# The second block of a two-block layer rebuilt: state rows exchanged by TensorE, queries and keys with features on partitions, attention output normed with tokens on partitions

## The chip, the cores and the metric

The kernel runs on one core of a Trainium2 chip. A core has TensorE (PE), VectorE (DVE), ScalarE (ACT), GpSimd (POOL) and SyncE (SP), which only issues transfers here. The metric is the device time of one launch in microseconds; the median of the runs counts. The profile is of one execution.

## The reference, cut to what matters

Two transformer blocks run on 512 tokens of width 1024 in fp32. The first is a hybrid of four token mixers with a gated FFN. The second, on which the change works, is this, with a modulated norm before each half:

```python
h = _rms(x, norm1_w) * (1 + sc1) + sh1
u, q, k, v = jnp.split(h @ w_in, [512, 1024, 1152], axis=-1)
y_ssm = _s5(u, ...)            # 32 groups of 16 channels, 64 complex states
q = _rms(q.reshape(b, s, 8, 64), q_norm_w)      # per head
k = _rms(k.reshape(b, s, 2, 64), k_norm_w)
y_attn = _swa_sink(q, k, v, rel_bias, sinks)    # window 128, blocks of 128 queries
mixed = jnp.concatenate([_rms(y_ssm, out_norm_ssm), _rms(y_attn, out_norm_attn)], axis=-1)
x = x + g1 * (mixed @ w_out)
h2 = _rms(x, norm2_w) * (1 + sc2) + sh2
x = x + g2 * _conv_ffn(h2, w_up, conv_w, conv_b, w_down)

# _s5: s[t] = a * s[t-1] + B u[t] (complex), y = Re(C s) + D * u
z = jax.nn.gelu(y)
return z * jax.nn.sigmoid(z @ w_glu + b_glu)

# _swa_sink, per head and query block of 128 over 256 keys
m = max(max(logits), sink); p = exp(logits - m)
out = (p / (sum(p) + exp(sink - m))) @ v
```

## The kernel before

A matrix product in fp32 accuracy is three passes of TensorE: each operand is split into a high and a low part (whi, wlo for weights, the two halves of an hl tile for activations), and hi·hi, lo·hi, hi·lo are added in PSUM. `proj_f` (L447) gives 128 output features on partitions by 512 tokens (24 matmuls of 512 columns for a width of 1024), `proj_t` (L476) gives tokens on partitions.

In time the program is: block 1 with its FFN until about 735 us; the middle of block 2 from there to about 940 us; the last FFN to the end. While the first FFN runs, "fillers" (L1227) compute tables for the state-space part (S5) and the modulation vectors.

The middle consists of steps, each a Python function that issues work for all engines. On TensorE the steps run in the order of the string ORDER, under `manual_schedule` (L1648). On the other engines the scheduler places the instructions. The steps, with the letters of ORDER before the change:

- U (`u_last`): the last projection of u. u goes to DRAM (d_u) and comes back as `ua`, 16 loads on POOL's queue, with channels of a group and 8 tokens on partitions.
- a, b, c, d (`s5_a` to `s5_d`), for each quarter q of the 32 groups: `a` multiplies ua by the table et (8 matmuls); `b` rotates the states (VectorE with real and imaginary halves crossed, `crossed`, POOL for one product) and scans them along the chunks of 8 tokens; `c` rotates back; `d` multiplies ua by tt and the states by gt (16 matmuls), sends the result through DRAM (d_z) to bring channels on partitions (yt), and adds D·u.
- e (`s5_e`): gelu and the split for the GLU. g (`glu`): w_glu, sigmoid as tanh, product, sum of squares. R (`norm_s`): the norm's scale.
- kp, qp: keys, values and queries with tokens on partitions; the head norms on VectorE (`head_norm`, L513 to L530, tile tokn); kt, qt: transposes to k2T, q2T.
- s, t, v (`swa_s`, `swa_t`, `swa_v`): for each of 8 pairs of a key head and a query block: scores, bias and row minimum on VectorE (L1577), exponentials on ScalarE (L1584), division on VectorE (L1587), transposes of the probabilities, and the product with v, with output features on partitions. Squares are summed into tot_a.
- p (`ssm_out`): the S5 half of the out-projection plus x, which is loaded again from d_x. A (`norm_a`): the attention norm's scale r_a. Then the attention half (`product`, finished by `w_out2`: scale by r_a on VectorE L1658, add L1659) leads over to the last FFN.

PSUM: three banks "acc", two "sc", two "tr", one "pv" (tile po). The constants NW2, NTAB are numbers of SBUF buffers; EN is a string that says for each copy or square whether ScalarE (a) or VectorE (v) does it.

Of the kernel before, what the change touches and what calls it, by code (L numbers as in the profile page):

```python
# [17 lines left out]
P = 128  # L18
# [23 lines left out]
HP = ""  # L42
EG = 0
EN = "avaaavaaaaaaaaaaaaavvvvvvvavavvaaaavaaaaaaaaaaaavaavvvvavvvvaaaavvvvaavvvaaaaavavaaavaavvavvvvvvvvvvavvaavvvvvavvaaavaaaavaaavvaaaaaaavvvvvvvaaaaaaaaavvvavvaavaaaav"
EN_AT = {'k1': (0, 4), 'v1': (4, 4), 'q1': (8, 12), 'h1': (20, 8), 'w1': (28, 8), 's1': (36, 8), 'o1': (44, 16), 't1': (60, 46), 'u2': (106, 4), 'z2': (110, 4), 'y2': (114, 4), 'k2': (118, 2), 'v2': (120, 2), 'q2': (122, 4), 'h2': (126, 12), 's2': (138, 12), 't2': (150, 14)}
ORDER = "U kp0 kp1 a0 a1 kt0 b0 qp0 c0 a2 b1 qp1 kt1 b2 c1 d0 a3 c2 qt0 qt1 b3 c3 d1 s0 qp2 s1 s2 t0 d2 t1 d3 e0 s3 e1 qt2 t2 s4 qp3 v0 t3 s5 v1 g0 qt3 g1 g2 t4 g3 s6 v2 v3 s7 t5 R p0 p1 v4 p2 t6 v5 p3 p4 v6 t7 p5 v7 p6 p7 A"
# [6 lines left out]
NW2 = 19  # L53
START = {0: lambda wc, wk: (wc[0].load(), wk[0].load())}
KSQ = 4
ZC = "bc"
# [8 lines left out]
def _rng(*r):  # L65
# [59 lines left out]
def pvec(i):  # L125
# [17 lines left out]
    o["ssm_d"] = _fv(z(i["ssm_d_2"])[0])  # L143
# [42 lines left out]
BLOCK1 = ("dist", "nlm", "distc", "rsum", "bd")  # L186
# [14 lines left out]
def arrays_of(i):  # L201
# [9 lines left out]
    for n in ("k", "v"):  # L211
# [9 lines left out]
        [np.concatenate(q) for q in ((br, bi), (bi, br), (cr, ci), (ci, cr))], axis=1))  # L221
    rb = g("rel_bias_2")
# [8 lines left out]
def build(tc, I, out, PV, PVN, CS, CSN, CS1, CSN1):  # L231
# [815 lines left out]
    d_g = [dpool.tile([P, 1152], F32, name=f"d_g{q}") for q in range(4)]  # L1047
# [24 lines left out]
    def s5_tables():  # L1072
# [72 lines left out]
        for n in range(8):  # L1145
            cmul(ro_r[:, n + 1], ro_i[:, n + 1], ro_r[:, n], ro_i[:, n], ro_r[:, n], ro_i[:, n], [P, 32], V)
# [231 lines left out]
    def tab(nm):  # L1378
        return bp.tile([P, 1024], F32, tag="tab", bufs=6, name=nm)
# [365 lines left out]
```

## Time and profile before

| | us |
|---|---|
| median of three runs | 1325.03 |
| lowest and highest | 1323.76, 1325.33 |
| the profiled execution | 1322.91 |
| its span on the core | 1321.2 |
| TensorE busy | 1242.7 (94% of the span) |
| VectorE busy | 840.3 (64%) |
| ScalarE busy | 551.5 (42%) |

The profiled execution is 2.1 us below the median. Its trace gives each instruction with its engine, source line, tile names, shapes and the idle time before it, with what ended that idle time. fp32 matmuls (those that aren't in three passes) count as two instructions each. A start-to-start distance says what an instruction costs in a row of its like; its own duration is longer, since matmuls overlap.

### The profile page before, as it was taken

The numbers are of one execution on the slowest core, as the hardware profiler recorded it, in microseconds if no ns is written. First come the engines' busy times: TensorE is split into PE (matmuls) and PEld (weight loads), VectorE is DVE, ScalarE is ACT, GpSimd is POOL, SyncE is SP. The second block draws the span as 40 slices with busy tenths as digits, with TensorE's granted clock in tenths as the row PEclk, the third lists the DMA queues.
The fourth block names the chain that finished last, engine by engine and source line by source line (L and its number), as shares of the span: only waits on it lengthen the run. The fifth ranks groups of instructions, "written<-read, shape, count | busy, mean of one in ns | idle before, by whom it ended". The sixth has DMA issues, their size and how long they took to land.

```text
span 1321.2 us, 17322 instructions
## 1 busy us (share of the span) xinstructions
PE 1242.7 (94%) x6269; PEld 999.7 (76%) x6269; DVE 840.3 (64%) x1615; ACT 551.5 (42%) x916; POOL 322.5 (24%) x403
## 2 busy tenths in 40 slices
PE   7999999999989879999999997889889999999998
PEld 6888765667867657778888986758868788888887
DVE  7668768777988878745445768775736353434362
ACT  5334466445223112322233442775655544444430
POOL 3000004012327439092511133014121212121200
PEclk8999999999999889999999987889989999999999
DMA  6431111126567676643434775277397979595921
GB/s 214 138 126 49 50 32 49 50 78 198 156 211 243 197 238 197 192 156 109 139 109 157 273 187 156 80 162 145 67 185 139 219 155 188 127 190 124 192 85 64
DMA packets 210869, 192.44 MB, mean 146 GB/s; under 512 B 13024, under 2 KB 173680, under 8 KB 210784
## 3 DMA queue, kind: packets, MB, share of 16 engines
q1 hardware_dynamic: 154240, 146.43, 36.5%
q0 software_dynamic: 51456, 40.61, 19.3%
q10 hardware_dynamic: 5088, 4.29, 1.0%
q8 instruction: 50, 0.82, 0.3%
q14 instruction: 35, 0.29, 0.1%
HBM read 177.70 MB, written 15.43 MB: 146 GB/s over the span
## 4 chain that ended last, share of the span: by engine, by line
PE 53%; DVE 12%; DMA 11%; issue 4%; ACT 2%; POOL 1%; ACTq 0%; DVEq 0%; POOLq 0%
PE acc L259 33%; PE sc L259 10%; PE tr L259 9%; DMA wm<-in_wmod_dram 7%; DVE wm L1065 3%; DVE wlo L371 2%; DMA wlo<-in_w_dram 1%; PE po L259 1%; DMA raw<-in_w_dram 1%; DVE hd L498 1%; DMA ua<-d_u 1%; PE tr L1595 1%; DVE z L1457 1%; DVE z L1446 1%; DVE z L1445 0%
## 5 line engine op out<-in xcount | busy, mean ns | idle before, releaser
L259 PE MATMUL acc<-hl,whi 128*128 128x512 f32 (+1 forms) x1624 | 487.1, 383 | 18.5 <-ACT whi L365 7.2
L259 PEld LDWEIGHTS acc<-hl,whi 128*128 128x128 f32 x1624 | 296.7, 190 | 87.6 <-issue 18.1
L365 ACT ACTIVATE whi<-raw 128x1024 fp32r<-128x1024 f32 (+1 forms) x187 | 193.9, 1039 | 365.8 <-PE acc L259 192.8
L259 PE MATMUL acc<-hl,wlo 128*128 128x512 f32 (+1 forms) x812 | 309.7, 382 | 1.7 <-DMA wlo<-in_w_dram 1.6
L371 DVE TENSOR_TENSOR wlo<-raw,whi 128x1024 fp32r<-128x1024 f32 (+1 forms) x133 | 177.7, 1338 | 61.2 <-ACT whi L365 58.4
L259 PEld LDWEIGHTS acc<-hl,wlo 128*128 128x128 f32 x812 | 153.9, 190 | 33.9 <-issue 4.4
L259 PE MATMUL acc<-hd,whi 128*128 128x512 f32 (+1 forms) x472 | 148.5, 398 | 17.2 <-DVE x L1327 11.0
L369 POOL DMA_DIRECT2D wlo<-in_w_dram x54 | 72.0, 1334 | 320.6 <-ACT wlo L368 216.7
L259 PEld LDWEIGHTS acc<-hd,whi 128*128 128x128 f32 x472 | 89.1, 194 | 40.7 <-DVE x L1327 9.2
L259 PE MATMUL acc<-whi,hl 128*128 128x256 f32 (+1 forms) x544 | 109.0, 291 | 1.9 <-ACT tok L246 1.6
L1065 DVE CUSTOM_DVE_ANT_0 wm<-wm,cb 128x512 f32<-128x512 f32 x96 | 81.1, 864 | 32.5 <-DMA wm<-in_wmod_dram 31.1
L259 PEld LDWEIGHTS acc<-whi,hl 128*128 128x128 f32 x544 | 89.2, 195 | 6.8 <-ACT tok L246 3.0
L259 PE MATMUL acc<-hd,wlo 128*128 128x512 f32 (+1 forms) x236 | 93.5, 396 | 0.0
L259 PE MATMUL acc<-wlo,hl 128*128 128x256 f32 (+1 forms) x272 | 78.9, 290 | 0.5 <-DVE wlo L371 0.5
L259 PE MATMUL tr<-hl,whi 128*128 128x512 f32 (+1 forms) x240 | 74.6, 394 | 0.0
L259 PE MATMUL sc<-hl,whi 128*128 128x512 f32 x208 | 64.9, 393 | 0.0
L368 ACT ACTIVATE wlo<-raw 128x1024 fp32r<-128x1024 f32 x54 | 56.5, 1046 | 3.9 <-PE acc L259 2.0
L259 PEld LDWEIGHTS acc<-wlo,hl 128*128 128x128 f32 x272 | 53.0, 195 | 2.6 <-DVE wlo L371 1.0
L918 POOL TENSOR_SCALAR_AFFINE_SELECT keep<-keep 128x128 f32<-128x128 f32 x16 | 9.3, 594 | 185.1 <-ACT keep L912 184.3
L259 PEld LDWEIGHTS acc<-hd,wlo 128*128 128x128 f32 x236 | 45.8, 194 | 9.9
L259 PEld LDWEIGHTS tr<-hl,whi 128*128 128x128 f32 x240 | 45.7, 193 | 10.1
L259 PE MATMUL tr<-hl,wlo 128*128 128x512 f32 (+1 forms) x120 | 47.5, 396 | 6.1 <-DMA wlo<-in_w_dram 6.1
(423 smaller groups left out, 1957.6 us busy)
## 6 DMA issues: line engine op xcount, KB each, us to landing
raw<-in_w_dram SPq DMA_DIRECT2D x177, 512.0 KB, 4.3
wlo<-in_w_dram POOLq DMA_DIRECT2D x54, 512.0 KB, 7.8
wm<-in_wmod_dram SPq DMA_DIRECT2D x96, 256.0 KB, 4.0
xk<-in_xT_dram SPq DMA_DIRECT2D x16, 256.0 KB, 4.7
d_g<-s5g POOLq DMA_DIRECT2D x4, 576.0 KB, 4.3
gt<-d_g SPq DMA_DIRECT2D x4, 576.0 KB, 5.7
w1c<-in_w1k_dram SPq DMA_DIRECT2D x8, 256.0 KB, 5.3
w1c<-in_w1v_dram SPq DMA_DIRECT2D x8, 256.0 KB, 6.6
```

Of the source, the lines that this page charges most:

```text
L259: nc.tensor.matmul(o, lhsT=l, rhs=r, start=start, stop=stop, **k)
L365: act(hi[:, :m], raw[:, :m], AF.Copy)
L368: act(lo[:, :m], raw[:, :m], AF.Copy, scale=-1.0)
L369: nc.gpsimd.dma_start(v(lo), self.src[:, k0:k1, c0:c1], accum_op=ALU.add)
L371: V.tensor_tensor(lo[:, :m], raw[:, :m], hi.bitcast(F32)[:, :m], op=ALU.subtract)
L498: V.tensor_tensor(dst[:, 1], src, dst.bitcast(F32)[:, 0], op=ALU.subtract)
L918: G.affine_select(g[:, d], g[:, d], fill=1.0, **past)
L1065: V.tensor_tensor_reduce(wm, wm, cb[:, n * 512:(n + 1) * 512], 1.0, 0.0, ALU.mult, ALU.add, mh[:, n, j:j + 1])
L1446: V.scalar_tensor_tensor(dst[im], src[re], -sign, t[re], op0=ALU.mult, op1=ALU.mult)
L1457: V.tensor_tensor_scan(z2[:, c], mag8[:, q * 8 + g:q * 8 + g + 1].to_broadcast([P, 64]), z[:, c], 0.0, ALU.mult, ALU.add)
L1595: nc.tensor.transpose(tp[:, m * P:(m + 1) * P], probs[n][:, hh, (j - j0) * P:(j - j0 + 1) * P], ident)
```

## The change

S5: `a` now makes, beside the states, the same states with real and imaginary halves exchanged, by two matmuls of half height per group. VectorE multiplies both from PSUM by cos and sin, adds, scans, and multiplies by cos and sin again; the return crossing is left out, and `d` instead takes a second product, with a table gs that is gt with its halves exchanged (24 matmuls in place of 16). D·u is put into the table tt by 32 small matmuls in the first FFN's fillers. The four quarters are collected in one tile za, and one gelu runs over all.

Attention: k, v and q are projected with features on partitions; squares on ScalarE, a sum over each head by a matmul with a block-diagonal matrix, and a scale by VectorE give k2T and q2T without transposes; only v is transposed. Scores of a query block are made for all eight heads in one step. Probabilities are not divided; the product with v has tokens on partitions, VectorE divides there, the norm is per token, and `swa_o` transposes the normed output. A (norm_a) and the scale r_a in `w_out2` are gone. The addition of x in `ssm_out` goes from POOL to VectorE.

The order string before and after:

```diff
-ORDER = "U kp0 kp1 a0 a1 kt0 b0 qp0 c0 a2 b1 qp1 kt1 b2 c1 d0 a3 c2 qt0 qt1 b3 c3 d1 s0 qp2 s1 s2 t0 d2 t1 d3 e0 s3 e1 qt2 t2 s4 qp3 v0 t3 s5 v1 g0 qt3 g1 g2 t4 g3 s6 v2 v3 s7 t5 R p0 p1 v4 p2 t6 v5 p3 p4 v6 t7 p5 v7 p6 p7 A"
+ORDER = "U k v kn a0 q0 vt a1 q1 qn0 a2 d0 q2 qn1 a3 d1 q3 qn2 d2 qn3 d3 s0 s1 t0 e s2 v0 t1 v1 g0 s3 t2 g1 o0 v2 g2 t3 g3 v3 R o1 p0 p1 p2 p3 p4 p5 p6 p7"
-NW2 = 19
+NW2 = 18
+NTAB = 9
```

The core of the rest:

```diff
+                mm(kp[r0:r0 + 16, c0:c0 + 16], ident[0:16, 0:16], dsk[:, d0:d0 + 16], False, True, skip_group_check=True)
...
     def s5_a(q):
-        pw = acc()
+        if q < 2:
+            s5_load(q + 2)
+        pw, px = tr(), tr()
         for g in range(8):
-            mm(pw[:, g * 64:g * 64 + 64], ets[q][:, g * P:(g + 1) * P], ua[:, q * 8 + g], True, True)
-        zs[q] = wt("z")
-        copy("z2", q, zs[q], pw)
+            c, u = slice(g * 64, g * 64 + 64), ua[:, q * 8 + g]
+            mm(pw[:, c], ets[q][:, g * P:(g + 1) * P], u, True, True)
+            for r0 in (0, 64):
+                mm(px[r0:r0 + 64, c], ets[q][:, g * P + 64 - r0:g * P + 128 - r0], u, True, True, skip_group_check=True)
+        z, z2 = wt("z"), wt("z2")
+        V.tensor_tensor(z, pw, cs[q], op=ALU.mult)
+        V.tensor_tensor(z2, px, ss[q], op=ALU.mult)
+        V.tensor_tensor(z, z, z2, op=ALU.add)
...
+        wc, wx = z, wt("wx")
+        V.tensor_tensor(wc, z2, cs[q], op=ALU.mult)
+        V.tensor_tensor(wx, z2, ss[q], op=ALU.mult)
...
+            mm(py[:, g * 64:g * 64 + 64], tts[q][:, g * P:(g + 1) * P], ua[:, q * 8 + g], True, False, skip_group_check=True)
+            mm(py[:, o], gts[q][:, g * P:(g + 1) * P], wc[:, c], False, False, skip_group_check=True)
+            mm(py[:, o], gss[q][:, g * P:(g + 1) * P], wx[:, c], False, True, skip_group_check=True)
...
+    def s5_e():
+        ge = act(za[0], za[0], AF.Gelu_apprx_tanh)
+        tables(ge)
...
+    def qkv_p(key, j, m):
         ps = acc()
-        for u in range(2):
-            proj_t(ps, wkv[0], h, 2 * n + u, 256, 256 * u)
+        proj_f(ps, wkv[j], h, m)
+        sq = wt("sq")
+        act(sq, ps, AF.Square)
...
+        mm(p2, C("bd"), sq, True, True)
+        rg = wt("rg")
+        rsqrt_m2(bp, ("w", NW2), rg, p2)
+        V.scalar_tensor_tensor(dst, ps, gcol[g], rg, op0=ALU.mult, op1=ALU.mult)
...
-        V.tensor_tensor(pr[:, :, :W], pr[:, :, :W], sl.unsqueeze(2).to_broadcast([P, 4, W]), op=ALU.mult)
...
+                mm(po[:, hh * 64:hh * 64 + 64], pvs[i, j, kv][:, a * P:(a + 1) * P], v2[:, j, 64 * kv:64 * kv + 64],
+                   j == j0 and hh == 0, j == i, skip_group_check=True)
...
-        t = wt("xa")
-        V.scalar_tensor_tensor(t[:, cs], ps[:, cs], gm[:, k:k + 1], r_a[:, cs], op0=ALU.mult, op1=ALU.mult)
-        V.tensor_tensor(x[k][:, cs], x[k][:, cs], t[:, cs], op=ALU.add)
+        V.scalar_tensor_tensor(x[k][:, cs], ps[:, cs], modT[:, 16 + k:17 + k], x[k][:, cs], op0=ALU.mult, op1=ALU.add)
```

How instructions move, at three places. First TensorE at an s5 input step, before (cst is the identity for transposes, tokn a normed query tile):

```order
L259 MATMUL acc<-whi,hl 128x256
L259 MATMUL acc<-ua,et 128x64 x16
L1528 MATMUL tr<-cst,tokn 128x128 x4
L259 MATMUL acc<-whi,hl 128x256
L259 MATMUL acc<-wlo,hl 128x256
L259 MATMUL acc<-whi,hl 128x256 x2
```

And after, from the end of the v projection, with the k norm (sc) and the first input step:

```order
L259 MATMUL acc<-hl,wlo 128x512
L259 MATMUL sc<-sq,cst 128x512
L259 MATMUL tr<-ua,et 128x64
L259 MATMUL tr<-ua,et 64x64 x2
L259 MATMUL tr<-ua,et 128x64
L259 MATMUL tr<-ua,et 64x64 x2
```

The input step was one run of whole matmuls; now whole ones and pairs of half-height ones alternate, and the transposes of normed tiles are gone.

Second, ScalarE's order around the gelu, before (prob are exponentials of one block of four heads, yt is one quarter of the S5 output):

```order
L1582 ACTIVATE se<-se 128x4
L1584 ACTIVATE prob_7449,sl<-prob_7449,ml 128x256 x4
L502 ACTIVATE nr<-nss,eps 128x8
L1493 ACT_TABLE_LOAD
L1493 ACTIVATE yt<-yt 128x512
L503 ACT_TABLE_LOAD
L503 ACTIVATE nr<-nr 128x8
L1582 ACTIVATE se<-se 128x4
L1584 ACTIVATE prob_7473,sl<-prob_7473,ml 128x256 x4
L497 ACTIVATE hl<-yt 128x512
```

And after (za is all of the S5 output, the second pt is a copy of transposed probabilities of query block 1, prob_7503 and prob_7504 belong to block 1, prob_7569 and prob_7570 to block 2):

```order
L1574 ACTIVATE prob_7504,sl<-prob_7504,ml 128x256 x4
L246 ACTIVATE pt<-tr 128x512
L1490 ACT_TABLE_LOAD
L1490 ACTIVATE za<-za 128x2048
L309 ACT_TABLE_LOAD
L501 ACTIVATE hl<-za 128x512 x4
L1571 ACTIVATE se<-se 128x8
L1574 ACTIVATE prob_7569,sl<-prob_7569,ml 128x256 x4
L1574 ACTIVATE prob_7570,sl<-prob_7570,ml 128x256 x4
L1606 ACTIVATE sq,ya_s<-ya 128x512
L246 ACTIVATE pt<-tr 128x512
```

The gelu of one quarter between exponentials has become one gelu of all four, with its two table loads, four splits and the next block's exponentials standing between two copies of block 1's transposes.

Third, SyncE's queue at the S5 tables, before (raw are weights, et, co, si, tt the tables):

```order
L353 DMA raw<-in_w_dram 128x8x128 x4
L353 DMA raw<-in_w_dram 128x1024
L1387 DMA et<-d_et_3111 128x1024
L1389 DMA co<-d_rot_3119 128x512
L1390 DMA si<-d_rot_3119 128x512
L1387 DMA et<-d_et_3112 128x1024
L1389 DMA co<-d_rot_3120 128x512
L1390 DMA si<-d_rot_3120 128x512
L1395 DMA tt<-d_t_3124 128x1024
```

And after, the last two of eight loads of x and what follows them:

```order
L1645 DMA x_6_8132<-d_x 128x512
L1645 DMA x_7_8150<-d_x 128x512
L1396 DMA et<-d_et_3112 128x1024
L1398 DMA co<-d_rot_3120 128x512
L1399 DMA si<-d_rot_3120 128x512
L1396 DMA et<-d_et_3113 128x1024
L1398 DMA co<-d_rot_3121 128x512
L1399 DMA si<-d_rot_3121 128x512
```

The loads of x stood behind the d_z stores of the last output step; now all eight stand ahead of the first table.

## Rows read from the trace of the kernel before

**Rows 1.** The page: TensorE's granted clock in 40 slices of 33 us.

```profile
PEclk8999999999999889999999987889989999999999
```

**Rows 2.** Busy time by stretch, from first to last us, all engines.

```profile
core 0: us, PE busy (x) PEld busy (x) DVE busy (x) ACT busy (x) POOL busy (x), PEclk, DMA share, GB/s
754.90:911.30 156.40, 135.17 (x828) 116.31 (x827) 110.63 (x269) 82.75 (x178) 42.32 (x49) 0.86 0.59 148
838.00:911.30 73.30, 63.84 (x344) 47.63 (x344) 48.26 (x124) 51.39 (x108) 15.55 (x15) 0.93 0.57 136
770.00:775.00 5.00, 4.65 (x24) 4.25 (x23) 2.29 (x4) 2.94 (x4) 0.79 (x2) 0.52 0.87 224
```

**Rows 3.** Waits of TensorE, 754 to 912: total, times, longest.

```profile
PE tr L1528 <- DVE tokn L530: 6.5, 1, 6.5
PE sc L259 <- DVE ml L1577: 6.5, 3, 5.0
```

**Rows 4.** Timeline of TensorE: start us, us, line, out<-in, shape, count, idle before.

```profile
749.28 0.71 PE L259 MATMUL acc<-hl,whi 128*128 128x512 f32 x2 [0.17 <-DVE uT L248]
...
754.91 0.28 PE L259 MATMUL acc<-whi,hl 128*128 128x256 f32 x1
...
768.34 3.92 PE L259 MATMUL acc<-ua,et 128*128 128x64 f32 x25 [1.99 <-DMA raw<-in_w_dram]
...
835.42 0.39 PE L259 MATMUL acc<-sp,gt 128*128 128x64 f32 x2
...
837.65 0.39 PE L259 MATMUL acc<-sp,gt 128*128 128x64 f32 x2
...
849.02 0.65 PE L259 MATMUL po<-pt,v 128*64 128x256 f32 x4
849.61 1.09 PE L1595 MATMUL tr<-cst,prob 128*128 128x128 f32 x8
850.63 1.14 PE L259 MATMUL sc<-k2T,q2T 64*128 64x256 f32 x8
851.70 1.08 PE L259 MATMUL po<-pt,v 128*64 128x256 f32 x8
...
911.34 1.03 PE L259 MATMUL acc<-hl,whi 128*128 128x512 f32 x2
```

**Rows 5.** Timeline of ScalarE, 820 to 865, same columns.

```profile
821.30 0.39 ACT L1584 ACTIVATE prob<-prob,ml 128x128 f32<-128x128 f32 x1
...
825.39 1.28 ACT L1493 ACT_TABLE_LOAD   x1
826.69 0.63 ACT L1493 ACTIVATE yt<-yt 128x512 f32<-128x512 f32 x1
...
829.82 0.49 ACT L1584 ACTIVATE prob<-prob,ml 128x256 f32<-128x256 f32 x1
...
856.62 0.57 ACT L246 ACTIVATE pt<-tr 128x512 f32<-128x512 f32 x1
```

**Rows 6.** Timeline of POOL, 752 to 775.

```profile
756.48 4.47 POOL L1424 DMA_DIRECT2D ua<-d_u  x8 [24.30 <-DMA d_u<-uT]
766.35 4.43 POOL L1424 DMA_DIRECT2D ua<-d_u  x8 [5.40 <-issue]
```

**Rows 7.** The chain that ended last, 905 to 942: start us, us, what.

```profile
911.05 0.86 PE sc L259 x2
...
934.53 0.40 DVE xa L1658
...
935.25 0.35 DVE x L1659
```

**Rows 8.** Timeline of SyncE's DMA issues, 715 to 745.

```profile
720.73 1.89 SPq L1387 DMA_DIRECT2D et<-d_et  x1
```

**Rows 9.** Timeline of VectorE, 733 to 746.

```profile
742.59 0.88 DVE L1341 SCALAR_TENSOR_TENSOR hm<-x,a,r 128x256 f32<-128x256 f32 x2
```

**Rows 10.** Timeline of TensorE in the first FFN, 404 to 408.

```profile
405.60 0.63 PE L259 MATMUL sc<-s5g,bb 128*16 128x128 f32 x16
```

More of the change, by code (lines that the diff above doesn't have):

```diff
@@ L1046, in build @@
     d_et = [dpool.tile([P, 1024], F32, name=f"d_et{q}") for q in range(4)]
-    d_g = [dpool.tile([P, 1152], F32, name=f"d_g{q}") for q in range(4)]
+    d_g = [dpool.tile([P, 1024], F32, name=f"d_g{q}") for q in range(4)]
     d_rot = [dpool.tile([P, 2, 512], F32, name=f"d_rot{q}") for q in range(4)]
@@ L1408, in build @@
     wkv = [weights("w5", 2 + j) for j in range(3)]
-    ua = bp.tile([P, 32, 64], F32, name="ua")
+    ua = bp.tile([P, 32, 64], F32, tag="ua", bufs=1, name="ua")
     v2 = bp.tile([P, NT, 128], F32, name="v2")
-    k2T = [wt(f"k2T{a}") for a in range(2)]
+    k2T = wt("k2T")
     q2T = [wt(f"q2T{a}") for a in range(4)]
@@ L1487, in s5_d @@
-        zT.append(yt)
-    def s5_e(n):
-        if EG and n == 0:
-            return
-        for q in (range(4) if EG else (2 * n, 2 * n + 1)):
-            ge = act(zT[q], zT[q], AF.Gelu_apprx_tanh)
+            E.dma_start(d_z[q].rearrange("g h t c -> t h g c")[t], ys[16 * t:16 * t + 16].rearrange("p (g c) -> p g c", g=8))
+        if q == 3:
+            za[0] = bp.tile([P, 4, S], F32, tag="ua", bufs=1, name="za")
+            for n in range(4):
+                yt = za[0][:, n]
+                nc.gpsimd.dma_start(yt, d_z[n].rearrange("g h t c -> (g h) (t c)"))
+                zT.append(yt)
@@ L1539, in build, with v_p, v_t @@
+    def v_p():
+        ps = acc()
+        proj_f(ps, wkv[0], h, 1)
+        held["v"] = vT = wt("vT")
+        act(vT, ps, AF.Copy)
+    def v_t():
+        tp = tr()
+        for t in range(NT):
+            nc.tensor.transpose(tp[:, t * P:(t + 1) * P], held["v"][:, t * P:(t + 1) * P], ident)
+        act(v2.rearrange("p t x -> p (t x)"), tp, AF.Copy)
     mixed = [hl() for _ in range(8)]
     relbs, probs, pvs = {}, {}, {}
-    tot_s, tot_a, r_s, r_a = (wt(n) for n in ("tot_s", "tot_a", "r_s", "r_a"))
+    tot_s, r_s = wt("tot_s"), wt("r_s")
@@ L1588, in swa_s, with swa_t @@
[L1588 to L1591 removed]
+        probs[i] = pr, sl
+    def swa_t(i):
+        j0, W = window(i)
         for j in range(j0, i + 1):
[L1593 to L1615 removed]
@@ L1618, in glu, with swa_o @@
+    def swa_o(n):
+        for b in range(2):
+            tp = tr()
+            for k in range(2):
+                for u in range(2):
+                    nc.tensor.transpose(tp[:, (2 * k + u) * P:(2 * k + u + 1) * P],
+                                        ya[2 * n + u][:, (2 * b + k) * P:(2 * b + k + 1) * P], ident)
+            for k in range(2):
+                split_scaled_to(mixed[4 + 2 * b + k], tp[:, k * 256:(k + 1) * 256], gcol["out_attn", 2 * b + k], HALVES[n])
     def glu(k):
@@ L1650, in build @@
             name = step.rstrip("0123456789")
-            with tc.high_priority() if name in HP.split(",") else nullcontext():
+            if name == "v" and step != name:
+                swa_v(int(step[1:]))
+            else:
                 steps[name](*([int(step[len(name):])] if step != name else []))
```

259 lines of the change are left out of this document (109 added, 150 removed).

## The prediction

> **What bounds the kernel now.** I read the page first for where TensorE is not at its peak: its clock row is below full speed in the middle of the program and in the slices around 740 to 900 us [rows 1]. That is the stretch which the change rewrites, so I take it as the unit: from the end of the last projection of u, 754.91, to the first matmul of the attention half of the out-projection, 911.34 [rows 4], 156.4 us. In it TensorE is busy 135.2 us at a mean granted clock of 0.86 [rows 2], so it does some 135.2 × 0.86 = 116 us of full-clock work, and 40 us are lost: 21 idle, 19 to the lower of the two clock levels (1.2 instead of 2.4 GHz). The waits say what the idle time waits for: 6.5 us for one normed q tile that VectorE makes, 6.5 us for VectorE's minima of the scores, and 2.0 us at the first use of ua, which the row puts down to a weight transfer although the next work needs only ua and a table [rows 3, 4]. After that 2.0 us wait the clock is 0.52 for 5 us [rows 2]. So the middle is bound by TensorE work plus the holes that VectorE's chains tear into it. ScalarE is busy 51 of the last 73 us [rows 2]: no bound now, but not free.
>
> **The change, stage 1: from 754.9 to the end of the last s5 output step (d3).** Six projections of 24 matmuls at 512 columns take 754.91 − 749.28 = 5.6 us each [rows 4], 33.8 (they replace as many half-width ones at the same work). Five block-diagonal norm matmuls at 0.9 (two fp32 instructions of 512 columns took 0.86 in the chain [rows 7]): 4.5. Four v transposes, half of the eight that took 1.02 [rows 4]: 0.5. The output step now has 24 instead of 16 fp32 matmuls of 64 columns per quarter; ten such took 837.65 − 835.42 = 2.23 [rows 4], 0.223 each, so 96 × 0.223 = 21.4. The input step has per quarter 8 whole matmuls (0.223) and 8 pairs of half-height ones for the swapped rows. No row shows such a pair. Bounds: 0.22, if both halves run side by side as the 64-high po matmuls do (four of 256 columns took 1.08 with their tail [rows 4], some 0.25 each), and 0.6, if they run one after the other and each change of form costs as at an entry to po: two matmuls alone took 0.59, against 2 × 0.25 in a run [rows 4], so 0.1 for in and out. I take side by side plus that 0.1, rounded up, 0.35, since po is the only row of two halves together. That makes 32 × (0.223 + 0.35) = 18.3, with ends 14.2 and 26.3. Sum: 78.5 us of TensorE work.
>
> By the Trainium skill (page "TensorEngine Tiling (Array Packing)", section "Key Properties") a change of tiling mode drains TensorE, while different tiles can work at once. Here every pair is a change and a change back, 64 times in all. The trace agrees with both halves of that as far as po goes; a drain as long as one matmul would put the pair at the upper end and the sum 8 us higher.
>
> Losses in stage 1. The first two s5 input steps still need ua. k, v and the k norm give 12.1 us of cover, to 767.0; before, the cover ended at 766.3 and the first step ran at 768.34 [rows 4]. POOL issues the loads at 756.48 and 766.35 [rows 6], and the change doesn't touch this path, so I leave 2 us of wait and the half clock that followed it, some 7 us at about 0.52 (5 of them are the row of [rows 2]), 3.5 lost. One more microsecond: the swapped rows now live in the two banks that the v transposes use as well, and the second input step waits until these are copied. d3 then ends at 754.9 + 78.5 + 6.5 = 839.9. What is removed here (z copies, crossed multiplies, POOL products, head norms) was in VectorE's holes, and VectorE's work per quarter falls to three products, eight scans and two products, under 5 us against a 20 us quarter: the tokn and sp waits are gone.
>
> On SP's queue the eight loads of x (2 MB) now stand ahead of the s5 tables, and they need buffers that the modulated rows of block 1 hold till 743.4 [rows 9]. The first table, issued at 720.73 before [rows 8], then goes out some 23 us later. It is used at 768, so I price that at nothing; the cover is about 15 us, and if the extra 3 MB before 765 delay ua too, up to 8 us show.
>
> **Stage 2: d3 to the first out-projection matmul.** TensorE: scores 24 × 0.27 + 8 × 0.16 = 7.7, 56 transposes at 0.13 = 7.4, 56 probability matmuls of 64 columns at 0.223 = 12.5 (before 28 wide ones in pairs), GLU 48 × 0.233 = 11.1, 16 y transposes 2.1, one norm 0.9: 41.7. ScalarE does everything that the scores feed, in a fixed order, and in the same stretch: 24 exponentials of 256 columns at 0.49 and 8 of 128 at 0.39 (14.9), the gelu of 2048 columns (1.95, an estimate: four of 0.63 less three starts), six table loads at 1.28 (7.7), 14 copies of the transposes at about 0.5 of which ScalarE does 7 (3.4) [rows 5], and sigmoids, squares, splits and weight conversions in like sizes (16.7, an estimate): 44.7 us, after about 3.2 us in which the first scores pass VectorE. Before, this work lay beside stage 1; now all of it stands behind d3. So stage 2 can't be shorter than about 48, and in order it is longer. I walked ScalarE's order against TensorE's: exponentials of blocks 0 and 1 till 11.2; one transpose copy; table, gelu, table till 16.2; four splits till 18.3; exponentials of block 2 till 22.3; the square of y0; and only then, 23.4, the second transpose copy of block 1. The next pair of transposes needs its bank, so TensorE stands from about 14.7 to 23.5. Behind such a hole the clock was 0.5 in this trace (0.52 after the 2.0 us wait [rows 2]), so I let the next 9 us of work run at half: block 1's products end at 32.4 instead of 28. Then GLU 0 to 36, scores 3 to 40, transposes 2 to 42.6, exponentials 3 to 46.4, GLU 1, y0 and y1 out, products 2 to 50, GLU 2 to 52.8; two table loads for one norm on ScalarE till 55.9; transposes 3 to 60.7, GLU 3, products 3 to 67.1, norm 69.9, y out 71.3. First out-projection matmul: 71.4 after d3.
>
> **Stage 3.** Eight out-projection steps of 12 matmuls: 8 × 2.8 = 22.2 (four of these were filled with attention work before). VectorE takes over POOL's eight additions of x here, in a stretch in which TensorE paces it.
>
> Sum: the attention half starts at 839.9 + 71.4 + 22.2 = 933.5 instead of 911.34, +22.2. The tail loses one of two VectorE steps per row tile: 0.40 and 0.35 stood in the chain [rows 7], about −1. In FFN1 32 matmuls of 16 × 16 (64 instructions) are added; 16 instructions of the nearest kind took 0.5 [rows 10], 2 us for 64 of these and less for the narrower ones: 1.5, ends 0.5 and 7. The probability scaling on VectorE that is gone ran beside TensorE's GLU and transposes: 0. Profile: 1322.9 + 22.2 − 1 + 1.5 = 1345.6. The median of the runs is 2.1 above the profiled execution (1325.0 against 1322.9): 1347.7, I say 1347.
>
> **The rivals.** *ScalarE never starves TensorE, faster.* If the scheduler's order is not felt because the exponentials run early (VectorE and ScalarE have little to do in the last output steps) and stage 2 costs 52, and if stage 1 keeps its 78.5 without wait or half clock, the attention half starts at 754.9 + 78.5 + 1 + 52 + 22.2 = 908.6: −2.7 − 1 + 1.5, 1320.7 in the profile, 1323 in the median; with pairs at 0.22 4 less, 1319. It decides at 13.5 us of losses in both stages together (156.4 − 142.4, less the 0.5 of the rest). For: far fewer steps cross from TensorE to VectorE and back. Against: ScalarE's 48 us alone leave 6 us of room. Chance 0.14. *Even:* the same with a few microseconds of holes, 0.08. *Much slower:* loads late by 8, pairs at 0.6 (+8), and stage 2 at half clock throughout (+10): 1347 + 26 = 1373. For: each hole was followed by half clock. Against: three things at once. Chance 0.13. My case, with losses of about 21 to 51 us, has 0.65, its own range 1332 to 1362. That the change does not do what it says (the pairs don't save VectorE time) only moves it inside these.
>
> **How the numbers follow.** Range 1320 to 1368: below it lies half of the fast case, above it half of the much slower one. Faster by over 0.2% (under 1322.4; about what a measurement of this kernel can tell from no change) 0.13, within 0.2% 0.09, slower 0.78.
>
> **What would show it.** TensorE's wait list from 755 to the product: tokn gone, a wait of some 9 us on ScalarE's transpose copy with the gelu ahead of it, clock 0.5 after it; the input step at 4.6 us per quarter; d3 at about 840; the attention half at about 933. Wrong if d3 ends before 836, or if no wait of stage 2 is over 3 us: then the fast case holds. Wrong the other way if an input step takes over 6 us or d0 waits for tables.

## The result and the profile after

The changed kernel takes 1382.9 us (median of four runs, 1380.5 to 1384.4) against 1324.4 for the kernel before on the same chip: 1.043 times as long, 95% interval 1.041 to 1.046. The forecast was 1347, so the sign was right and the size was not; the time lies outside the range of 1320 to 1368. One execution of this study, the profiled one of the run pxg (2458.9 us, against 1369.1 in its other run), was in a slow state of the chip and is not read; the same kernel was run again as pxg_b.

The profiled execution took 1381.5 us (span 1379.8), 58.6 more than the one of before. Four points of TensorE's timeline split that. They are the same ones that the prediction used: the end of the last u projection, the end of the last S5 output step (d3), the first out-projection matmul, the first matmul of its attention half.

| us | before | after, measured | after, forecast |
|---|---|---|---|
| to the end of the u projection | 754.9 | 772.6 | 756.4 |
| stage 1, to d3 | | 101.8 | 85.0 |
| stage 2, to the out-projection | | 78.2 | 71.4 |
| stage 3, to its attention half | | 23.0 | 22.2 |
| the three together | 156.4 | 203.0 | 178.6 |
| from there to the end of the span | 409.9 | 404.2 | 408.9 |

So +17.7 us came in the first FFN, +46.6 in the middle, and 5.7 were given back in the last FFN. The first FFN took 16 us more than forecast, stage 1 17 more, stage 2 7 more, the last FFN 5 less.

The stretches of the changed kernel, columns as in [rows 2] (first FFN, stage 1, stage 2, and a piece of stage 1):

```profile
320.00:772.64 452.64, 422.65 (x1951) 337.15 (x1950) 296.79 (x556) 128.30 (x181) 158.22 (x256) 0.97 0.55 170
772.64:874.43 101.79, 87.59 (x543) 71.34 (x542) 37.03 (x74) 29.46 (x40) 13.43 (x22) 0.88 0.82 203
874.43:952.60 78.17, 59.33 (x299) 48.00 (x299) 37.56 (x128) 50.80 (x127) 3.87 (x6) 0.73 0.16 38
815.00:820.00 5.00, 5.00 (x31) 3.92 (x30) 0.00 (x0) 0.00 (x0) 0.77 (x1) 0.50 1.03 285
```

In stage 1 TensorE stands 14 us and runs below full clock for part of the rest (0.50 at 815 to 820), while the DMA engines are at 0.82 over the stretch and at 1.03 in that piece. In stage 2 it is the other way round: DMA at 0.16, VectorE busy for half and ScalarE for two thirds, TensorE idle for 19 us and at a mean clock of 0.73, which makes 43 us at full clock of its 59 (59.33 × 0.73).

TensorE's longest waits in the middle, the answer to [rows 3]:

```profile
PE tr L1585 <- ACT pt L246: 7.0, 3, 6.5
PE acc L259 <- ACT whi L365: 5.7, 1, 5.7
PE tr L1585 <- DVE hl L498: 5.3, 2, 3.1
PE tr L1525 <- DVE z L1455: 4.5, 1, 4.5
PE sc L259 <- DVE ml L1567: 4.0, 6, 0.9
```

tokn and sp are gone, as forecast, and the wait of 6.5 us for a transpose copy (forecast: some 9) is there. The lines with whi and z are stage 1's, with a third wait, of 4.0 us for v: 14.2 us together. The forecast had 1 us for v's and none for the others; the 2 us that it had for ua did not come. Where they stand in time (timeline of TensorE, the answer to [rows 4]; x46 are the rest of the second input step, a quarter of the groups):

```profile
784.03 1.22 PE L259 MATMUL acc<-hl,whi 128*128 128x512 f32 x2 [5.69 <-ACT whi L365]
...
807.70 0.69 PE L1525 MATMUL tr<-cst,vT 128*128 128x128 f32 x4 [4.51 <-DVE z L1455]
...
812.87 7.72 PE L259 MATMUL tr<-ua,et 128*64 128x64 f32 x46 [3.97 <-ACT v L1526]
```

### The profile page after: what moved, and what is told of

Its sections match the earlier page's. It is cut to its first block, busy times and chain, and to the rows that moved or that the text cites. A ratio compares the mean times of both kernels' runs of the same rounds, so it can differ in the third digit from the quotient of the medians.

```text
span 1379.8 us, 17573 instructions
## 1 busy us (share of the span) xinstructions
PE 1287.7 (93%) x6441; PEld 1025.9 (74%) x6441; DVE 802.1 (58%) x1554; ACT 555.6 (40%) x913; POOL 282.9 (21%) x383
## 4 chain that ended last, share of the span: by engine, by line
PE 51%; DMA 10%; issue 9%; DVE 8%; POOL 3%; ACT 3%; ACTq 0%; POOLq 0%; DVEq 0%; SPq 0%
PE acc L259 28%; PE sc L259 10%; PE tr L259 10%; DMA wm<-in_wmod_dram 5%; DVE wm L1069 2%; DMA raw<-in_w_dram 2%; DVE wlo L371 2%; PE po L259 1%; DMA wlo<-in_w_dram 1%; DMA tt<-d_t 1%; POOL wlo L369 1%; ACT prob L1574 1%; ACT whi L365 1%; DMA d_et<-s5et 0%; POOL s5t L1089 0%
## 5 line engine op out<-in xcount | busy, mean ns | idle before, releaser
L259 PE MATMUL acc<-hl,whi 128*128 128x512 f32 (+1 forms) x1720 | 522.3, 387 | 23.9 <-ACT whi L365 12.7
L259 PEld LDWEIGHTS acc<-hl,whi 128*128 128x128 f32 x1720 | 318.8, 193 | 94.6 <-issue 16.8
L259 PE MATMUL acc<-hl,wlo 128*128 128x512 f32 (+1 forms) x860 | 331.0, 385 | 4.9 <-DMA wlo<-in_w_dram 4.8
L371 DVE TENSOR_TENSOR wlo<-raw,whi 128x1024 fp32r<-128x1024 f32 (+1 forms) x133 | 167.4, 1260 | 79.6 <-ACT whi L365 76.7
L259 PEld LDWEIGHTS acc<-hl,wlo 128*128 128x128 f32 x860 | 165.1, 192 | 40.7 <-issue 4.5
L259 PE MATMUL acc<-whi,hl 128*128 128x256 f32 (+1 forms) x352 | 72.5, 293 | 1.6 <-ACT tok L246 1.6
L259 PEld LDWEIGHTS acc<-whi,hl 128*128 128x128 f32 x352 | 58.2, 195 | 5.6 <-ACT tok L246 3.0
L1703 DVE SCALAR_TENSOR_TENSOR cf<-acc,pv,cf 128x511 f32<-128x511 f32 (+1 forms) x34 | 25.1, 747 | 51.2 <-ACT cf L1701 50.7
L259 PE MATMUL acc<-wlo,hl 128*128 128x256 f32 (+1 forms) x176 | 51.3, 292 | 0.6 <-DVE wlo L371 0.6
L1337 DVE TENSOR_TENSOR x<-x,acc 128x512 f32<-128x512 f32 (+1 forms) x49 | 31.9, 654 | 27.4 <-PE acc L259 27.2
```

The lines of the kernel that those rows point to most:

```text
L259: nc.tensor.matmul(o, lhsT=l, rhs=r, start=start, stop=stop, **k)
L371: V.tensor_tensor(lo[:, :m], raw[:, :m], hi.bitcast(F32)[:, :m], op=ALU.subtract)
L1337: V.tensor_tensor(x[k][:, cs], x[k][:, cs], ps[:, cs], op=ALU.add)
L1703: V.scalar_tensor_tensor(t[:, b:S], ps[:, 0:S - b], V1("conv_w2", 3 * k + 2 - b), t[:, b:S], op0=ALU.mult, op1=ALU.add)
```

## The experiments

The stages in all kernels, from the profiled execution of each, by the same points of TensorE's timeline. The first line of the body is the changed kernel itself. Kernels that are alike up to the u projection reached it between 771.0 and 775.6 (the all6 kernels between 751.7 and 757.1). Kernels alike in a stage differ by 3.2 us in stage 1 (changed, dskg, sign, ptv) and by 3.7 in stage 2 (changed, dskg, sign, pxg_b, xlate), and once by 6 (stage 1 of all6sc). Smaller differences say nothing. The medians come from several chips, on which the kernel before took 1324.4 (changed), 1325.9 (dskg, sign, xlate), 1324.2 (vtsc, ptv, all6), 1324.5 (nogelu) and 1320.6 (the others). dskg, sign, xlate, vtsc, ptv and nogelu have two runs each, up to 11 us apart (xlate 1372.4 and 1383.4), so the stages tell more than these medians.

| kernel | u projection ends | stage 1 | stage 2 | median of runs |
|---|---|---|---|---|
| changed | 772.6 | 101.8 | 78.2 | 1382.9 |
| dskg | 765.0 | 99.3 | 74.6 | 1371.8 |
| sign | 756.6 | 102.5 | 78.3 | 1370.4 |
| pxg_b | 773.2 | 90.9 | 77.4 | 1372.2 |
| xlate | 771.0 | 96.3 | 77.1 | 1377.9 |
| vtsc | 773.2 | 100.6 | 81.0 | 1379.5 |
| ptv | 775.6 | 100.4 | 78.0 | 1382.0 |
| nogelu | 775.3 | 108.3 | 83.3 | 1394.5 |
| all6 | 752.4 | 84.7 | 79.9 | 1346.7 |
| all6sc | 752.6 | 90.7 | 77.1 | 1346.3 |
| all6warm | 751.7 | 84.9 | 77.1 | 1344.2 |
| all6scwarm | 757.1 | 84.3 | 74.0 | 1343.8 |

### The first FFN: dskg and sign

```diff
# dskg: all table matmuls of a quarter, then all D-skip matmuls
             for g in range(8):
                 mm(kp[...], bb[:, g], gt[:, g, 0:8]..., True, False)
+            for g in range(8):
                 mm(kp[...], ident[0:16, 0:16], dsk[...], False, True)
# sign
-            V.tensor_scalar(rt[:, 1], rt[:, 1], sgn, -1.0, op0=ALU.mult, op1=ALU.mult)
+            G.tensor_scalar(rt[:, 1], rt[:, 1], sgn, -1.0, op0=ALU.mult, op1=ALU.mult)
```

> Only the order of the small matmuls in the first FFN's table fillers is changed: all 8 table matmuls of a quarter first, then all 8 of the D skip, instead of in turns. Theory A: what costs is the change of tile form at every matmul (a quarter took 3.69 us in the changed kernel, 0.56 before): a quarter now takes about 1.2 us, the last u projection ends some 10 us earlier than 772.6, the run takes about 1372. Rival B: the D-skip matmuls cost their 3 us by themselves (small, accumulating onto a sum just written): a quarter stays above 3 us and the run within 2 us of 1382.

> The sign of the sine table is applied on POOL, which makes the table, instead of on VectorE. Theory A: VectorE, working in order, stood 42 us waiting for POOL in the first FFN, and TensorE waited for the gate and residual steps behind it: the last u projection ends about 5 us earlier, the run takes about 1377. Rival B: these waits of VectorE are slack and the FFN's holes are those of before: no change over 1 us.

In the changed kernel the two kinds of small matmuls come in turns, eight times per quarter. First its timeline of TensorE, of the first pair and of what follows the last, then that of dskg (two blocks, the answer to [rows 10]):

```profile
405.35 0.39 PE L259 MATMUL sc<-s5g,bb 128*16 128x128 f32 x2
405.67 0.21 PE L259 MATMUL sc<-dsk,cst 16*16 16x16 f32 x2
...
409.04 0.73 PE L259 MATMUL acc<-hd,whi 128*128 128x512 f32 x2
```

```profile
405.03 0.63 PE L259 MATMUL sc<-s5g,bb 128*16 128x128 f32 x16
405.59 0.28 PE L259 MATMUL sc<-dsk,cst 16*16 16x16 f32 x16
405.80 0.73 PE L259 MATMUL acc<-hd,whi 128*128 128x512 f32 x2
```

In turns a quarter takes 409.04 − 405.35 = 3.69 us, in groups 0.77, for the same instructions, so theory A holds. In turns there are 17 changes of tile form, in groups three: if the saving of 2.92 us were theirs alone, the 14 that are left out would cost 0.21 us each. But grouping also lets matmuls that write different rows of the result start together. The first four instructions of a group start within 0.02 us (dskg, TensorE from 405.027 to 405.05), while in turns one matmul's two instructions stand alone, 0.12 us apart:

```profile
405.03 0.30 PE L259 MATMUL sc<-s5g,bb 128*16 128x128 f32 x4
```

No run separates the two. Four quarters are 11.7 us, and the u projection ended 7.6 earlier: TensorE's busy time up to it (from 320 us) fell by 8.5, at a mean clock of 0.95 instead of 0.97, and its idle time grew by 0.9.

sign gave 16.0, three times what theory A said. VectorE's instruction on the sine table stood in its queue until POOL had made the table (view of one line of the changed kernel: shapes and first and last start, then who was waited for):

```profile
L1233 DVE TENSOR_SCALAR s5r<-s5r,cst x4: 485/486/607, 420.0 to 665.5; 128x512 f32<-128x512 f32 x4
...
  POOL s5r L1090: 42.0, 4
```

Four instructions of half a microsecond cost VectorE 42 us of standing, and everything of the FFN that was queued behind them stood too. Without them TensorE's waits for VectorE in this FFN (first here the changed kernel, then sign; 320 to 745 us) fall from 29.8 to 17.3 us in all:

```profile
PE acc L259 <- DVE fg L1313: 13.7, 6, 4.3
PE acc L259 <- DVE x L1337: 12.1, 5, 3.5
```

```profile
PE acc L259 <- DVE x L1337: 9.9, 7, 3.0
PE acc L259 <- DVE fg L1313: 4.9, 2, 2.8
```

The two gains do not add up: together (all6) the projection ends at 752.4, 20 us earlier and not 24; a difference of that size is within the spread.

### Stage 1: pxg_b, xlate, vtsc

```diff
# pxg_b
             mm(pw[:, c], ets[q][:, g * P:(g + 1) * P], u, True, True)
+        for g in range(8):
+            c, u = slice(g * 64, g * 64 + 64), ua[:, q * 8 + g]
             for r0 in (0, 64):
                 mm(px[r0:r0 + 64, c], ...)
# xlate, in ssm_out
         x[k] = xp.tile([P, S], F32, tag="x", name=f"x4_{k}")
+        V.tensor_copy(x[k][:, 0:1], v2[:, 0, 0:1])
         nc.sync.dma_start(x[k], d_x[k])
# vtsc, in v_t
-        tp = tr()
+        tp = sc()
```

> In the s5 input step the 8 whole matmuls come first, then the 16 half-height ones. Theory A (the change of form costs): a step falls from 4.94 to about 3.6 us, 8 x 0.22 and 8 x 0.22 for halves side by side; d3 comes 5 us earlier, run about 1377. Rival B (the halves run one after the other): a step stays at 4.9 and the run at 1382.

> The changed kernel with the whole matmuls of an input step first and the half-height ones behind them (the earlier run of this edit was disturbed; in the six edits together a step took 2.9 us instead of 4.9). Theory A: the step's 2.0 us come off four times, d3 is 6 to 8 us earlier after the last u projection than the 101.8 of the changed kernel, run about 1374. Rival B: the input steps lie behind waits for tables, so the gain is eaten by longer waits: stage 1 within 3 us of 101.8.

> The eight loads of x get a write into their tile (one column, from the transposed v) ahead, so they cannot be issued before the v transposes; nothing else moves. Theory A: they hold up SP's queue and the DMA engines, so that the weights of v, the tables and ua come late: v's wait of 5.7 us goes, the tables land by the first input step, and with the half clock behind these holes d3 comes 8 to 16 us earlier; run 1366 to 1374. Rival B: the traffic of the tables and weights alone fills the DMA engines from 760 to 800: d3 moves by under 3 us, run about 1380.

> The v transposes write into a bank of the score pool instead of the pool that the input steps use. Theory A: v's transposes stood 4.5 us for the first input step's products to be read and the second input step 4.0 us for the copy of v, because three users share two banks: both waits go (4 us of them at least, since the second input step still needs both banks read once), and part of the half clock behind them; d3 6 to 12 us earlier, run about 1373. Rival B: the two waits are the same late cosine tables and weights seen twice, so one wait of about 8 us stays in front of the second input step; run within 3 us of 1382.

The first two are of the same kernel, pxg and pxg_b; pxg_b is read here.

**pxg_b:** stage 1 is 10.9 us shorter. An input step with the first matmul behind it, in the changed kernel and in pxg_b:

```profile
829.15 5.00 PE L259 MATMUL tr<-ua,et 128*128 128x64 f32 x48
834.09 0.43 PE L259 MATMUL acc<-ua,tt 128*128 128x64 f32 x2
```

```profile
837.70 2.98 PE L259 MATMUL tr<-ua,et 128*128 128x64 f32 x48
840.61 0.43 PE L259 MATMUL acc<-ua,tt 128*128 128x64 f32 x2
```

2.91 us instead of 4.94: 8 × 0.223 for the whole matmuls leaves 0.14 for a pair of half-height ones in a row, against 0.395 in turns. In turns there are 16 changes of form, in groups two; the 14 that are saved cost 0.145 each (the two halves of a pair start 0.007 us apart in both kernels, so nothing else changed). That is 8 of the 10.9 us; the rest is within the spread. Theory A holds, and more than it said, as a pair costs less than a whole matmul. The Trainium skill says of this (page "TensorEngine Tiling (Array Packing)", section "Key Properties") that changing the tiling mode drains TensorE and that tiles work independently; the trace fits both, with 0.145 us a change and halves that start 0.007 us apart.

**xlate:** stage 1 is 5.5 us shorter. In the changed kernel SP's queue held the loads of x until their buffers, those of the modulated rows hm, came free (its waits from 715 to 800; then its timeline, start, duration, transfers, the answer to [rows 8]):

```profile
SPq L1645 <- DVE hm L1351: 19.3, 4, 17.3
```

```profile
756.23 5.62 SPq L1645 DMA_DIRECT2D x<-d_x  x8
761.90 0.42 SPq L1396 DMA_DIRECT2D et<-d_et  x1
...
774.87 1.29 SPq L353 DMA_DIRECT2D raw<-in_w_dram  x2
```

The first table went out at 761.90, 41 us later than before and not 23. So the weights of v went out at 774.9 at the earliest, behind 2 MB of x and the tables, and ScalarE, which splits them, shows the wait that TensorE then had:

```profile
782.92 1.06 ACT L365 ACTIVATE whi<-raw 128x1024 fp32r<-128x1024 f32 x1 [15.28 <-DMA raw<-in_w_dram]
```

With the x loads behind, TensorE's wait for whi is gone, and in its place comes one of 1.4 us for ua (xlate, waits of TensorE from 766 to 868):

```profile
PE tr L259 <- ACT v L1526: 3.8, 1, 3.8
PE tr L1525 <- DVE z L1455: 2.4, 1, 2.4
PE tr L259 <- DMA ua<-d_u: 1.4, 1, 1.4
```

The gain lies between the 8 us that theory A said at least and the 3 of rival B. 6.2 us of the other two waits stayed, and SP's queue now stood 20.0 us in front of the sine table, for VectorE, so v's weights went out only 8 us earlier (766.8).

**vtsc** was to show what these two waits are. With v's transposes in another bank the waits for z and v in front of the second input step are 0.8 us together, and TensorE's idle time in stage 1 falls from 14.2 to 4.8. Yet stage 1 is only 1 us shorter (columns as above):

```profile
773.26:873.78 100.52, 95.68 (x543) 78.82 (x542) 37.21 (x74) 29.44 (x40) 13.43 (x22) 0.83 0.82 204
```

TensorE needs 95.7 us instead of 87.6 for as many matmuls, at a mean clock of 0.83 instead of 0.88. So rival B's time came out but not its wait of 8 us, and theory A's waits went but not its time: the lower clock took the gain back. That this can happen without any edit shows in ptv, whose stage 1 is that of the changed kernel: its wait for z is 0.2 us and its stage 1 100.4. What the banks cost stays open. In all6, where VectorE's queue can be read without the other losses, it stands until 780.3 for the low part of a weight that ScalarE's split has to precede, which waits for its transfer, and only then reads the input step's products (timeline of VectorE); TensorE shows it as 4.0 us for z.

```profile
780.32 1.23 DVE L371 TENSOR_TENSOR wlo<-raw,whi 128x1024 fp32r<-128x1024 f32 x1 [3.46 <-ACT whi L365]
781.47 0.68 DVE L1460 TENSOR_TENSOR z<-tr,co 128x512 f32<-128x512 f32 x1
```

### Stage 2: ptv, nogelu, all6 and what was added to it

ptv puts two copies of block 1's transposes on VectorE; nogelu leaves the gelu out (its output is therefore another); all6 has the six edits dskg, sign, pxg, xlate, vtsc, ptv; all6sc and all6warm add one edit each to it, all6scwarm both:

```diff
# ptv: two letters of EN from a to v       # nogelu
-        ge = act(za[0], za[0], AF.Gelu_apprx_tanh)
-        tables(ge)
# all6sc, in swa_s
-            ps = [sc(), sc()]
+            ps = [sc(), sc()] if b == 0 else [acc(), acc()]
# all6warm: matmuls that nothing reads; warm(1) after each half of the scores,
# warm(8) between the two pairs of block 1's transposes
+    def warm(n):
+        dm = acc()
+        for _ in range(n):
+            mm(dm, q2T[0][:, 0:P], q2T[1], True, True)
```

> Two of the copies of transposed probabilities of query block 1 go from ScalarE to VectorE, so they do not stand behind the gelu. Theory A: the wait of 6.5 us of TensorE on that copy goes, and the products of block 1 come 6 us earlier; run about 1376. Rival B: the half clock and ScalarE's load in stage 2 take it back later (ScalarE is the bound there): less than 2 us are left at the first out-projection matmul, run about 1381.

> The gelu of the S5 output is left out of the changed kernel, and with it two table loads; the splits stay. Theory A: the gelu block of ScalarE is what TensorE's transposes of query block 1 wait for: their wait of 6.5 us shrinks to under 2 us, and the first out-projection matmul comes 5 to 8 us earlier after d3 (78.2 now). Rival B: ScalarE's exponentials and the half clock bound stage 2 anyway: under 3 us.

> All six edits together: D-skip matmuls grouped, sign on POOL, half-height matmuls grouped, x loads later, v transposes in a score bank, two copies on VectorE. If the losses add up: first FFN 17 us shorter, stage 1 about 80 to 84 instead of 101.8, stage 2 about 68 to 72 instead of 78, so 1330 to 1340. If they hide one another, 1350 or more.

> The six edits, and the second half of each block's scores goes to two of the three acc banks, so that TensorE needs not wait for VectorE's minima before it. Theory A: these waits (4.5 us) go and the half clock behind them: stage 2 from 78.9 to 70 or less, run about 1337. Rival B: the chain behind (exponentials, transposes) sets the pace: stage 2 stays above 76.

> The six edits, and idle matmuls (128 x 512, nothing reads them) where TensorE waits in stage 2: two in each score step, eight between the two pairs of transposes of block 1; some 14 us of work more at full clock. Theory A (half clock): TensorE stays at the higher level, stage 2 falls to 65 to 72 in spite of the added work. Rival B (latency of the chain): no gain, stage 2 78 to 90.

> Both of these edits on the six. If half clock and score banks each cost what theory A says, stage 2 is 60 to 68 and the run 1326 to 1334; if a chain through ScalarE and VectorE bounds it, 76 or more.

The forecast's picture of ScalarE's queue was right in its order. In the changed kernel the two copies of transposes stand on either side of table, gelu, table, splits, block 2's exponentials and the square of y0, and TensorE's transposes follow the second one. All of it lies on the chain of work that ended last (start, duration, what):

```profile
890.48 1.91 ACT za L1490
...
893.70 2.19 ACT hl L501 x4
895.89 0.10 ACT se L1571
895.99 3.93 ACT prob L1574 x16
899.92 0.61 ACT sq L1606 x2
900.53 0.49 ACT pt L246
```

TensorE's wait of 6.5 us ends with that copy. In **ptv** VectorE's first copy stands behind the second half of the same splits, which waits for ScalarE's first half (timeline of VectorE), and its second one behind the sums of block 2's exponentials:

```profile
895.84 2.50 DVE L502 TENSOR_TENSOR hl<-za,hl 128x512 fp32r<-128x512 f32 x4 [0.46 <-ACT hl L501]
898.25 0.69 DVE L248 COPY pt<-tr 128x512 f32<-128x512 f32 x1
```

TensorE then waits 5.1 us for VectorE instead of 6.5 for ScalarE, and stage 2 is 78.0; rival B's time came out. ptv's chain still passes the gelu. In **nogelu** the scheduler moves three splits ahead, where ScalarE stands 5.5 us for the transfer of za and holds up the last q norm; the copy still stands behind block 2's exponentials, the wait is 4.5, another of 4.5 for the last q norm is new, and stage 2 is 83.3, longer and not shorter. That run does not price the gelu, since it moved other work; it shows that the gelu isn't the only thing in front of the copy, as theory A would have it.

**all6** lands at 1346.7, 1.018 times the kernel before (1.014 to 1.022), between its two theories. The first FFN and stage 1 (84.7, the sum of the single gains) are as short as theory A said, and stage 2 is 79.9, as if nothing had been done there. **all6warm** asks whether the half clock is the bound. Its stretch of stage 2, then that of all6:

```profile
836.60:913.70 77.10, 65.60 (x331) 45.17 (x331) 40.17 (x131) 50.35 (x125) 3.92 (x6) 0.89 0.19 44
```

```profile
837.10:917.00 79.90, 59.62 (x300) 47.31 (x299) 39.72 (x131) 49.35 (x124) 3.86 (x6) 0.75 0.18 41
```

14 us of added work raised the clock from 0.75 to 0.89 and cost nothing: the stage is 2.8 shorter, within the spread, and theory A (65 to 72) falls. all6sc takes the waits for the score minima away and gives 2.8 as well, as its rival B said; its stage 1, where no line was edited, was 6 longer in that execution (it waited 6.8 us for z and 2.2 for a copy of S5 outputs). Both together give 5.9, to 74.0, between the two theories and not far over the spread. So neither the half clock nor the score banks alone hold the stage.

The chains say more about the gelu. In ptv, all6, all6sc, all6warm and all6scwarm the chain still passes the gelu block and block 2's exponentials (in all6 from 853.15 to 863.90). In nogelu, and in attnonly of the next section, it goes without the gelu block, from block 2's scores through VectorE's minima to the same exponentials (attnonly, d3 at 873.05):

```profile
894.90 2.15 ACT prob L1581 x9
897.05 0.61 ACT sq L1613 x2
897.66 0.49 ACT pt L247
```

The copy then starts 24.6 us after d3 instead of 26.1, and TensorE's wait for it is 4.7 us instead of 6.5. By that comparison the gelu block is some 2 us of the hole. What all these kernels have in common is that the copy stands behind block 2's exponentials (ptv's on VectorE behind their sums). In all6o1 of the next section block 1's copies come ahead of them and cost 1.3 us of waits, but TensorE then waits 7.2 us for a later copy, behind block 3's exponentials. So what that order is worth is not shown.

### Other orders, and each half of the change alone

> The six edits, and TensorE's order changed so that the scores, exponentials and transposes of query blocks 0 and 1 stand between the last three s5 output steps, and the gelu comes after block 3's scores. Theory A: stage 2 was long since all of ScalarE's work stood behind d3; now part of it lies beside d1 to d3: 8 to 12 us less than the six edits alone, 1320 to 1330. Rival B: the smaller cover for the tables and the banks takes that back: no gain over the six edits.

> The six edits, and a milder change of TensorE's order: both last q norms ahead of d2, the scores of block 0 between d2 and d3, scores and products of blocks 1 to 3 ahead of the GLU. Theory A: stage 2 falls by the 8 us of exponentials that now lie beside d3 and by the gelu's wait, 1330 to 1338. Rival B: the scheduler keeps the gelu between the exponentials and the banks are short, as with the stronger reordering: 1345 or more.

Only the order string of all6 differs: in all6o1 and all6o4 scores stand between the last S5 output steps.

```diff
-ORDER = "... q2 qn1 a3 d1 q3 qn2 d2 qn3 d3 s0 s1 t0 e s2 v0 t1 v1 g0 s3 t2 g1 o0 v2 ..."
+ORDER = "... q2 qn1 a3 d1 q3 qn2 qn3 d2 s0 d3 s1 t0 s2 v0 t1 v1 s3 t2 e v2 g0 t3 o0 ..."   # all6o4
+ORDER = "... q2 qn1 a3 q3 qn2 d1 qn3 s0 d2 s1 t0 d3 s2 t1 v0 v1 s3 t2 e v2 g0 t3 o0 ..."   # all6o1
```

They took 1352.3 and 1362.7, longer than all6. From the u projection to the out-projection all6 needs 164.6 us, all6o4 169.6, all6o1 177.1. A wait for the second input step's products (7.4 and 6.8 instead of 4.0) and one of 6.0 for the GLU's sum of squares, now at the end with little to cover it, take the place of the gain. Theory A falls for these two orders; others were not tried.

> The kernel before with the S5 half of the change alone: swapped rows by grouped half-height matmuls, three products and the scan on VectorE, 24 output matmuls per quarter; attention, D skip and gelu as before, the sine's sign on POOL. Its order string is that of before with the removed steps left out. Theory A (the S5 half moves work from VectorE to TensorE at about even price; the loss of the change lies elsewhere): 11.7 us more TensorE work, and the waits for tokn and sp and part of the half clock behind them go: 1318 to 1332. Rival B (the S5 half is what costs, by its extra tables on the DMA engines and its TensorE work): over 1340.

> The changed kernel with the S5 half of before put back (crossed multiplies on VectorE and POOL, D skip by VectorE, gelu in four pieces). Theory A (the attention half costs, since all of ScalarE's exponentials stand behind d3): stage 2 stays at 70 to 78 us, the first FFN is as short as before, stage 1 about 75: 1330 to 1345. Rival B (the attention half is fine without the gelu block and the late tables): stage 2 under 62, run under 1325.

s5only puts the new input and output steps (grouped) and the gs loads into the kernel before; attnonly puts the S5 steps of before into the changed kernel, with the order string `U k v kn a0 q0 vt a1 b0 q1 qn0 c0 a2 b1 d0 q2 qn1 c1 a3 b2 d1 q3 qn2 c2 b3 d2 e0 qn3 c3 d3 s0 ...`. s5only takes 1340.3, 1.014 times the kernel before (1.009 to 1.019), at the bound of rival B. Its middle is 175.3 instead of 156.4. 11.7 us of that are TensorE work as reckoned from the rows. There is also this wait for weights, which the kernel before doesn't have. SP's queue issues these weights at 754.8, behind the new gs tables of over 2 MB, and at 746.3 in the kernel before; no run took these tables away:

```profile
PE acc L259 <- ACT whi L365: 9.1, 1, 9.1
```

attnonly takes 1380.2, which neither theory said, and is no fair price of the attention half: 22.5 us of it are waits for sp, probably since its order gave the four-step S5 of before too little cover. Stage 2 is long again, 78.3, although the gelu is in four pieces and only one of them stands between block 1's copies.

No kernel of this study beat the one before. The best median of the changed line is all6scwarm's, 1343.8, 1.015 times the kernel before on its chip; with an interval of 1.011 to 1.019 it can't be told from all6.

## Why the prediction was wrong

**The first FFN, +17.7 instead of +1.5.** The step that failed is "in FFN1 32 matmuls of 16 × 16 are added". Their price came from a row of one kind of matmul in a run [rows 10], and they run in turns with another form: 12.5 us of TensorE instead of 1.5, beyond the upper end of 7. Worse, the new VectorE instruction on the sine table was not in the sum at all. It does 0.5 us of work, but it waits for POOL, and the question of what is queued behind it was not asked. sign shows that this was the larger part (16.0 us, against 7.6 by dskg).

**Stage 1's work, 78.5, was right.** The input step took 4.94 us (4.6 forecast); TensorE's 87.6 us at 0.88 are 77 at full clock. The value for a pair, 0.35, was near the 0.395 measured, and the reason, side by side plus a change of form, holds. That its size fits is partly luck: the pair itself is cheaper than forecast (about 0.11 instead of 0.25) and two changes of form are dearer (0.29 instead of 0.1).

**Stage 1's losses, 6.5 forecast, 23.3 measured.** The step that failed is the loads of x "at nothing". I asked when the first table is used (768) and found cover for it; TensorE did not wait for that table. What had no cover were the weights, v's first, further back in the same queue. xlate shows 5.5 us for the loads of x; in all6 the last late weight still costs 4.0 at z. The rival "loads late by 8" had the right queue, at 0.13, but meant ua, for which TensorE did not wait. The 14.2 us of waits brought half clock with them, as the prediction assumed of holes in general (0.50 at 815 to 820). How much of the rest is banks and how much late weights is open, since in vtsc the clock took back what the waits gave.

**Stage 2, 71.4 forecast, 78.2 measured.** The walk through ScalarE's queue gave the hole in the right place (14.7 to 23.5 after d3; measured 20 to 26.6), the two table loads of the y norm show as 5.3 us for hl, and TensorE's work was right (41.7 forecast, 43 measured). The term that was mis-sized is the half clock: 9 us of work at half, 4.5 lost, where the stage lost 16 (59.3 busy, 43 at full clock); its idle time, 18.8, was less than the 25 that the walk leaves (71.4 − 41.7 − 4.5). all6warm shows that the 16 can't simply be taken off: at 0.89 the stage still took 77.1. That the gelu makes the hole was mostly wrong too: with no gelu block on the chain 4.5 (nogelu) and 4.7 us (attnonly) of the 6.5 stay, behind block 2's exponentials. What bounds the stage stays open.

**The tail, −1 forecast, −5.7 measured.** The wait of 2.7 us for the first normed rows is gone, and waits for low weight parts went from 7.7 to 5.6 us. No run tells why the latter did.

With the six edits, all6 took 1346.7 where 1347 was forecast. That agreement is luck: all6 has grouped input steps, some 7 us cheaper than the forecast's, so its stage 1 of 84.7 (forecast 85.0) still holds 7 us more of losses, its stage 2 is 8 longer, and its first FFN 4 shorter.

**The gain that was hoped for went** first into work for TensorE, the engine that already bound this stretch: 142 us at full clock by the sum against 116. The fast rival needed under 13.5 us of losses to break even, and even all6 has some 50 (its middle takes 187 us, some 137 of them work).

## What to carry to other kernels

Of every instruction that a change adds to an in-order queue, ask first what it waits for and what stands behind it: four half-microsecond instructions cost some 16 us here, and eight loads that nobody needed yet some 5 of stage 1. Price small matmuls with the change of form between them, and put like ones in a row: that was worth 11 us in stage 1 and 8 in the first FFN. A wait seen in the trace in the place that was forecast is not yet the bound: it may move to another engine (ptv), or the clock may take back what it gave (vtsc). Before calling it the bound, take it away, and compare busy time and clock as well as waits.

## What was not expected of the hardware

A change between tile forms cost 0.145 us of TensorE (128 × 128 and 128 × 64). Between 128 × 16 and 16 × 16 it was at most 0.21 us, with what is lost because four matmuls no longer start together. In vtsc TensorE waited 9 us less in stage 1 and needed 8 us more for as many matmuls, as its mean granted clock was 0.83 instead of 0.88. 14 us of matmuls that nothing reads, put into waits, raised the mean granted clock of stage 2 from 0.75 to 0.89 (between the 1.2 and the 2.4 GHz level) at no cost in time, and without a gain clear of the spread.
